# State-space tiles in a frame centred on the 128 double steps, scanned once, and modulation sums by TensorE

## The chip, the cores and the metric

The kernel runs on one core of one Trainium2 chip. The metric is the device time of one execution in microseconds (us); the median of the runs shown is compared.

## The reference, cut to what matters

The model has two layers. Layer 0 mixes tokens with a diagonal complex state-space model (S5), layer 1 with a convolution; each is followed by a SwiGLU feed-forward net. Shift, scale and gate of each sub-layer are sums over the 2048 channels of the condition vector times a weight matrix.

```python
mod = c_act @ ada_w[i] + ada_b[i]                  # six rows of 2048: shift, scale, gate, twice
h = x * (1.0 + sc_m) + sh_m
# S5, for each of 128 groups of 16 channels, with 64 complex states:
a_bar = jnp.exp(lam * dt)
b_bar = ((a_bar - 1.0) / lam)[..., None] * b_mat
h_t = a_bar * h_(t-1) + b_bar @ u_t                # over 256 steps
y = real(c_mat @ h) ; y = gelu(y + d_skip * u)
vg = y @ w_glu ; y = vg[..., :d] * sigmoid(vg[..., d:])
```

The time axis has 256 steps; all matrices are float32.

## The kernel before, in words

**The state-space stage** takes the first part of the execution. A tile `ct` holds 128 channels (8 groups); there are 16 tiles. Two time steps are joined to one double step, so a scan runs over 128 double steps with the factor a_bar squared. A complex scan is made real by turning: with a squared factor of modulus rho and angle w, the input of double step c is multiplied by exp(-i w c), a real scan with rho runs over it, and the result is turned back by exp(i w c). The table of cosines and sines (`tab`) holds 64 entries for each pair of states. So the 128 double steps are cut into two halves `s` of 64, each in its own frame; the end of the first half is turned by 64 steps and added to the first input of the second half. That is the carry: `cx`, `cy`, with the factor `rw` (lines 468 to 477), between the scans of the first half (`step(0)`) and of the second (`step(1)`).

For a tile, `weights_in` turns the input matrices (`mb`, `lz`), `inputs` turns the 128 channels of `x` and applies shift and scale (`u` and `uh`), `drive` multiplies into PSUM (`pin`, 1024 numbers a partition, two banks), and `scan` does the work on VectorE: two multiplies by the table into `x1`, two in place into `pin`, an addition and a subtraction, four scans of 256, the carry, two multiplies into `pc` and two into `psn`. `read_out` multiplies `pc` and `psn` by the output matrices (`mc`) into `y`, after a matmul with the direct term (`bd`, `dd`), and `gelu` follows, in three parts put between the parts of the next scan (`between`). `tables` completes `tab` on GpSimd (POOL) and fills the scan's factors `rho` on ScalarE (ACT).

**Order.** PE's order is written out by hand (`manual_schedule`): in the loop over `ct`, weights of tile ct+1, read-out of tile ct-1, inputs and drive of ct+1, output weights of ct+1, and between them units of the modulation sums. The other engines run in the order that a planner chose when the program was built, each in order at run time.

**Modulation sums.** A unit is 1 MB of `ada_w`, loaded on SyncE's queue into one of six buffers, and multiplied on PE by the condition vector (L632). `plan` gives how many units go into each tile: 4, 4, 2, 2, then 3 for eight tiles, then 4 for four. After four units (two for the first four, narrower blocks) a block of 512 columns is done. Its four partial rows lie on partitions 0, 32, 64 and 96; ACT copies them (`adas`), PE turns each 128 columns by a transpose (`adat`, L640), VectorE sums the four (L643) and adds the bias (L644) into `mod`. Sixteen such blocks fall into this stage. From tile 15 on, the GLU projection's matmuls (L891) follow, with the last scan and the last read-outs between its units.

Of the kernel before, what the change touches and what calls it, by code (L numbers as in the profile page):

```python
# [155 lines left out]
class S5:  # L156
# [8 lines left out]
    def __init__(self, tc, const, ident, psum, psum_tag, psum2):  # L165
        self.psum2 = psum2
        self.tc, self.nc, self.ident = tc, tc.nc, ident
        self.psum, self.ptag = psum, psum_tag
        self.keep_ctx, self.work_ctx, self.mats_ctx = ExitStack(), ExitStack(), ExitStack()
        self.keep = self.keep_ctx.enter_context(tc.tile_pool(name="s5keep", bufs=1))  # L170

        self.cm = self.keep.tile([P, 4, NPAIR, GI], F32, name="cm")

        self.sel = self.keep.tile([P, 4, 2, 32], F32, name="sel")
        for q in range(4):
            self.nc.vector.tensor_copy(out=self.sel[:, q], in_=bc(ident[:, 32 * q:32 * q + 32], 1, 2))
# [5 lines left out]
        self.rw = const.tile([P, 2, NPAIR], F32, name="rw")  # L182
# [5 lines left out]
        self.bd = [w.tile([P, P], F32, name=f"bd{i}") for i in range(3)]  # L188
        self.dd = [w.tile([P, P], F32, name=f"dd{i}") for i in range(3)]
        self.rh = [w.tile([P, 2, 2, 2, 64], F32, name=f"rho{i}") for i in range(2)]  # L190
        for i in range(3):
            for m in (self.mb, self.mc, self.bd, self.rh):
                if i < len(m):
                    self.nc.gpsimd.memset(m[i], 0.0)
# [33 lines left out]
    def turn_mats(self):  # L228

        nc, cm = self.nc, self.cm  # L230
        for q in range(2):
            src = [n.rearrange("p (n i) -> p i n", i=GI) if q == 0 else n.rearrange("p (i n) -> p i n", i=GI)
                   for n in self.nat[2 * q:2 * q + 2]]
            for h in range(4):
                b = self.bank("turn")
                for i in range(4):
                    for r in range(2):
                        k = slice((2 * i + r) * 64, (2 * i + r) * 64 + 64)
                        for a in range(2):
                            nc.tensor.matmul(b[64 * a:64 * a + 64, k], src[r][:, 4 * h + i], self.ident[:, a::2], start=True, stop=True)  # L240
                bv = b.rearrange("p (i r j) -> p r i j", i=4, r=2)
                for r in range(2):
                    nc.scalar.activation(
                        out=cm[:, 2 * q + r, :, 4 * h:4 * h + 4].rearrange("p j i -> p i j"), in_=bv[:, r],
                        func=AF.Copy, scale=-1.0 if q == 1 and r == 1 else 1.0)
                yield

    def prep(self, pp):
# [20 lines left out]
        self.wt = wt[:, 1:]  # L269
# [10 lines left out]
        v.tt(rho, e, e, MUL)  # L280

        for i, l in enumerate((lr, li)):
            g.tt(wt[:, 0, i], l, rec, MUL)
        self.lam = [wt[:, 0, i] for i in range(2)]

    def factors(self):
# [7 lines left out]
        for out, x, y in zip(t, (am1, ai, ai, am1), (lr, li, lr, li)):  # L294
            v.tt(out, x, y, MUL)
        for r in range(2):
            last = v.tt(self.rw[:, r], self.wt[:, 6, r], rho, MUL)
# [4 lines left out]
    def matrices(self, q, engines):  # L302
# [3 lines left out]
        _, cfr, cfi, ar, ai = (bc(self.par[:, i, sl], 2, GI) for i in range(5))  # L306
        u = [keep.tile([P, 16, GI], F32, tag=f"mu{i}", name=f"mu{i}") for i in range(4)]
# [13 lines left out]
        steps = ((c[0:2], (ar, ai), 0, (SUB, ADD)), (c[2:4], (cfr, cfi), 2, (ADD, SUB)), (m[2:4], (ar, ai), 4, (ADD, SUB)))  # L321
# [9 lines left out]
    def quarter(self, q, eng):  # L331
# [3 lines left out]
        for r in range(2):  # L335
            eng.memset(t[:, r, :, 0:1], 1.0 - r)
# [21 lines left out]
    def tables(self, ct, behind=()):  # L358
# [42 lines left out]
    def weights_out(self, ct, skip, behind):  # L401

        nc, k = self.nc, ct % 4
        qc, mb, mc = self.qm[ct // 4][1], self.mb[ct % 2], self.mc[ct % 3]
        dd = self.dd[ct % 3]
# [8 lines left out]
        for r_, end in ((0, False), (1, True)):  # L414
            for p in range(4):
                r = slice(32 * p, 32 * p + 32)
                nc.tensor.matmul(
                    bk[r, 0:32], mb[:, r_, p, 1].rearrange("p a b -> p (a b)"), self.cols(ct, r_, p), start=False, stop=end)
        for p in range(4):
            r = slice(32 * p, 32 * p + 32)  # L420
            nc.scalar.copy(out=self.bd[ct % 3][r, r], in_=bk[r, 0:32])

    def drive(self, ct, u):
# [6 lines left out]
        pin = self.psum2.tile([P, 2, 2, 2, 2, 64], F32, tag="pin", name="pin")  # L430
        for h in range(2):
            for r in range(2):
                for a in range(2):
                    k = slice(64 * a, 64 * a + 64)
                    nc.tensor.matmul(pin[:, a, :, r, h], lz[k, h, r, :], u[k, h], start=h + r == 0, stop=h + r == 2)
        return pin

    def scan(self, ct, pin, tab, between):
# [18 lines left out]
        xf, pf = (z.rearrange("p a s r h c -> p (a s) r (h c)") for z in (x1, pin))
        v.tensor_tensor(out=pf[:, :, 1], in0=xf[:, :, 0], in1=pf[:, :, 1], op=ADD)
        v.tensor_tensor(out=pf[:, :, 0], in0=xf[:, :, 1], in1=pf[:, :, 0], op=SUB)

        def step(s):
            for a in range(2):
                z = pin[:, a, s].rearrange("p r h c -> p (r h c)")
                v.tensor_tensor_scan(out=z, data0=rh[:, a].rearrange("p r h c -> p (r h c)"), data1=z, initial=0.0, op0=MUL, op1=ADD)  # L464

        step(0)
        between()
        cx, cy = (w.tile([P, 2, 2, 2], F32, tag=n, name=n) for n in ("cx", "cy"))
        end = pin[:, :, 0, :, :, 63]
        rw = self.rw[:, :, 4 * ct:4 * ct + 4].rearrange("p k (h a) -> p k a h", a=2)  # L470
        v.tensor_tensor(out=cx, in0=end, in1=bc(rw[:, 0], 2, 2), op=MUL)
        v.tensor_tensor(out=cy, in0=end, in1=bc(rw[:, 1], 2, 2), op=MUL)
        between()
        v.tensor_tensor(out=cx[:, :, 0], in0=cx[:, :, 0], in1=cy[:, :, 1], op=ADD)
        v.tensor_tensor(out=cx[:, :, 1], in0=cx[:, :, 1], in1=cy[:, :, 0], op=SUB)
        first = pin[:, :, 1, :, :, 0]
        v.tensor_tensor(out=first, in0=first, in1=cx, op=ADD)
        between()
        step(1)
        pc, psn = (w.tile([P, 2, 2, 2, 2, 64], F32, tag=n, name=n) for n in ("pc", "psn"))  # L480
        turn(pc, 0)
        between()
        turn(psn, 1)
        return pc, psn

    def read_out(self, ct, u, pc, psn):
# [3 lines left out]
        nc.tensor.matmul(y[:, 0:HALF + 1], self.bd[ct % 3], u[:, 0:HALF + 1], start=True, stop=False)  # L490
        nc.tensor.matmul(y[:, SEQ:SEQ + HALF], self.dd[ct % 3], u[:, HALF:], start=False, stop=False)

        terms = ((0, pc, 1), (1, pc, 0), (2, psn, 0), (1, psn, 1))
        for k, (mi, src, r) in enumerate(terms):
            for tau in range(2):
                ids = {0: (2, 3, 5), 1: (0, 1, 4)}[tau]
                for p in range(4):
# [4 lines left out]
                        y[rr, o:o + HALF].rearrange("p (s c) -> p s c", s=2), self.cols(ct, ids[mi], p), src[:, p % 2, :, r, p // 2],  # L502
                        start=False, stop=tau == 1 and k == 3)
# [4 lines left out]
def kernel(  # L508
# [49 lines left out]
    s5 = S5(tc, const, ident, auxp, "aux", pin_ctx.enter_context(tc.tile_pool(name="pin", bufs=2, space=PSUM)))  # L558
    s5_prep = ExitStack()
# [64 lines left out]
    def ada_block(layer, j, c0, n):  # L624
# [13 lines left out]
        tr = aux("adat")[:, :n]  # L638
# [696 lines left out]
    def inputs(ct):  # L1335
# [445 lines left out]
```

## Time and profile before

| | |
|---|---|
| median of 3 runs | 2293.14 us (2290.69 to 2295.21) |
| the profiled execution | 2298.0 us, its span 2295.8 us |
| granted TensorE clock, mean | 0.992 |
| PE, DVE, ACT, POOL busy | 97%, 74%, 44%, 7% of the span |
| data moved | 579.48 MB, 252 GB/s over the span |

The profile is of one execution. PE is TensorE, DVE VectorE, ACT ScalarE, POOL GpSimd, SP SyncE; L452 is line 452 of the kernel. A tile's name stands for any of its buffers.

### The profile page before, as it was taken

What the parts mean: (1) busy time and instruction counts of PE and PEld (TensorE: products, weight loads), DVE (VectorE), ACT (ScalarE), POOL (GpSimd) and SP (SyncE); (2) the same over time, 40 slices, a digit from 0 to 9 for tenths busy, and PEclk for the clock granted to TensorE, in tenths of its full rate; (3) what the DMA queues carried; (4) which work ended last, traced back from release to release, by engine and by line L of the source; (5) the groups of instructions that cost most, each with busy time, mean ns of one, the idle gap of its engine ahead of it and who ended that gap; (6) DMA issues with size and microseconds to landing.
All of it is one profiled execution on the core that took longest, in us unless ns stands there. A gap on an engine that the chain in (4) does not pass through costs nothing.

```text
span 2295.8 us, 33563 instructions
## 1 busy us (share of the span) xinstructions
PE 2223.8 (97%) x13619; PEld 1799.3 (78%) x13619; DVE 1691.1 (74%) x1941; ACT 1015.6 (44%) x1253; POOL 156.0 (7%) x268
## 2 busy tenths in 40 slices
PE   6888999999999999999999998999999999999999
PEld 4555777987777887787898776898888888888888
DVE  8899888887787777787989788878755444545474
ACT  4665334644334333434446333556443333343343
POOL 5662000000000000000010110000000000000000
PEclk9999999999999999999999999999999999999999
DMA  9889799488998998999866774766875555565542
GB/s 333 288 298 301 270 329 347 161 300 310 321 320 323 325 323 308 324 323 322 307 203 195 213 214 163 276 206 203 291 234 190 188 191 189 184 193 191 185 166 92
DMA packets 380608, 579.48 MB, mean 252 GB/s; under 512 B 13875, under 2 KB 277939, under 8 KB 365987
## 3 DMA queue, kind: packets, MB, share of 16 engines
q1 hardware_dynamic: 379862, 576.82, 74.3%
q8 instruction: 107, 1.75, 0.3%
q0 software_dynamic: 352, 0.45, 0.1%
q14 instruction: 47, 0.39, 0.0%
q10 hardware_dynamic: 240, 0.08, 0.0%
HBM read 573.72 MB, written 3.57 MB: 251 GB/s over the span
## 4 chain that ended last, share of the span: by engine, by line
PE 69%; DVE 13%; DMA 9%; ACT 5%; issue 3%; SPq 0%; POOL 0%; DVEq 0%; ACTq 0%
PE acc L891 55%; PE acc L895 6%; DMA raw<-in_ffn_w_gu_dram 5%; DVE wlo L836 4%; ACT whi L835 3%; DVE adaacc L703 2%; DMA raw<-in_ffn_w_down_dram 2%; PE acc L1007 2%; PE turned L907 1%; PE conv L1672 1%; DMA raw<-in_s_w_glu_dram 1%; DVE pin L464 1%; PE y L501 1%; PE ada L632 1%; DMA raw<-in_ada_w_dram 1%
## 5 line engine op out<-in xcount | busy, mean ns | idle before, releaser
L836 DVE TENSOR_TENSOR wlo<-raw,whi 128x2048 fp32r<-128x2048 f32 x344 | 788.9, 2294 | 462.5 <-ACT whi L835 460.8
L835 ACT CAST whi<-raw 128x2048 fp32r<-128x2048 f32 x344 | 655.6, 1906 | 826.3 <-PE acc L891 407.1
L891 PE MATMUL acc<-whi,h 128*128 128x512 f32 x3648 | 889.2, 393 | 11.3 <-ACT whi L835 11.0
L891 PEld LDWEIGHTS acc<-whi,h 128*128 128x128 f32 x3648 | 677.3, 188 | 166.0 <-ACT whi L835 18.8
L891 PE MATMUL acc<-wlo,h 128*128 128x512 f32 x1824 | 461.7, 390 | 1.0 <-DVE wlo L836 0.9
L891 PEld LDWEIGHTS acc<-wlo,h 128*128 128x128 f32 x1824 | 341.6, 188 | 74.3 <-DVE wlo L836 3.7
L891 PE MATMUL acc<-whi,f 128*128 128x512 f32 x1248 | 300.9, 391 | 0.0
L703 DVE SCALAR_TENSOR_TENSOR adaacc<-rawa,c_act,adaacc 128x2048 f32<-128x2048 f32 (+1 forms) x135 | 284.5, 2107 | 0.4
L891 PEld LDWEIGHTS acc<-whi,f 128*128 128x128 f32 x1248 | 232.8, 188 | 49.5 <-ACT whi L835 1.7
L891 PE MATMUL acc<-wlo,f 128*128 128x512 f32 x624 | 156.4, 389 | 0.0
L891 PEld LDWEIGHTS acc<-wlo,f 128*128 128x128 f32 x624 | 117.1, 188 | 24.3
L1602 POOL TENSOR_TENSOR lw<-fold,wtap 128x1024 f32<-128x1024 f32 x12 | 26.3, 2195 | 1064.1 <-PE acc L895 874.8
L632 PE MATMUL ada<-raw,c_rep 128*32 128x512 f32 (+1 forms) x576 | 71.3, 591 | 5.7 <-DMA raw<-in_ada_w_dram 3.7
L1240 ACT ACTIVATE fsg<-acc 128x256 f32<-128x256 f32 x84 | 31.6, 379 | 96.2 <-PE acc L891 96.2
L895 PE MATMUL acc<-h,whi 128*128 128x256 f32 x512 | 67.3, 286 | 4.2 <-DVE h L1705 2.2
L895 PEld LDWEIGHTS acc<-h,whi 128*128 128x128 f32 x512 | 63.6, 192 | 9.9 <-ACT h L911 4.3
L1184 POOL CAST lnmh<-lno 128x2 fp32r<-128x2 f32 x1 | 0.2, 181 | 885.3 <-DVE lno L68 885.3
L1241 DVE TENSOR_TENSOR fsg<-acc,fsg 128x256 f32<-128x256 f32 x84 | 35.0, 418 | 16.0 <-ACT fsg L1240 16.0
L464 DVE TENSOR_TENSOR_SCAN pin<-rho,pin 128x256 f32<-128x256 f32 x64 | 44.2, 691 | 1.5
L1672 PE MATMUL conv<-vs,lw 128*32 128x256 f32 x720 | 42.2, 380 | 0.1
L895 PE MATMUL acc<-f,whi 128*128 128x256 f32 x320 | 40.7, 284 | 0.0
L895 PEld LDWEIGHTS acc<-f,whi 128*128 128x128 f32 x320 | 39.3, 192 | 0.2
(349 smaller groups left out, 1852.8 us busy)
## 6 DMA issues: line engine op xcount, KB each, us to landing
raw<-in_ffn_w_gu_dram SPq DMA_DIRECT2D x352, 512.0 KB, 4.7
rawa<-in_ada_w_dram SPq DMA_DIRECT2D x128, 1024.0 KB, 5.6
raw<-in_ffn_w_down_dram SPq DMA_DIRECT2D x88, 1024.0 KB, 5.1
raw<-in_ada_w_dram SPq DMA_DIRECT2D x64, 1024.0 KB, 7.6
raw<-in_s_w_glu_dram SPq DMA_DIRECT2D x64, 512.0 KB, 6.1
raw<-in_cv_w_pw_dram SPq DMA_DIRECT2D x64, 512.0 KB, 5.9
raw<-in_cv_w_pw_dram SPq DMA_DIRECT2D x16, 1024.0 KB, 5.9
vs<-scr SPq DMA_DIRECT2D x40, 142.0 KB, 5.5
```

The source lines that it names most:

```text
L464: v.tensor_tensor_scan(out=z, data0=rh[:, a].rearrange("p r h c -> p (r h c)"), data1=z, initial=0.0, op0=MUL, op1=ADD)
L632: nc.tensor.matmul(acc[32 * (k % 4):32 * (k % 4) + 32, :], c_rep[:, kk, :], r[:, k, :], start=kk < 4, stop=kk >= NCH - 4)
L703: nc.vector.scalar_tensor_tensor(out=acc, in0=r[:, i], scalar=c_act[:, kk:kk + 1], in1=acc, op0=MUL, op1=ADD)
L835: m1 = nc.scalar.copy(out=self.hi[:, :kn], in_=r[:, :kn])
L836: m2 = nc.vector.tensor_tensor(out=self.lo[:, :kn], in0=r[:, :kn], in1=self.hi[:, :kn].bitcast(F32), op=SUB)
L891: nc.tensor.matmul(acc[bank].rearrange("p a b -> p (a b)"), x[:, bank * HALF:(bank + 1) * HALF], wt[:, k], start=first, stop=end)
L895: nc.tensor.matmul(acc[bank][:, i], wt[:, k, m * P:(m + 1) * P], x, start=first and i == 0, stop=end and i == 1)
L1007: nc.tensor.matmul(acc[m][:, 0:EW], wt[:, k, m * P:(m + 1) * P], xx[:, 4 * u + k], start=u == 0 and n == 0, stop=u == 3 and n == len(order ...
L1240: nc.scalar.activation(out=t[:, i], in_=gv[:, 0], func=AF.Sigmoid)
L1241: nc.vector.tensor_tensor(out=t[:, i], in0=gv[:, 0], in1=t[:, i], op=MUL)
L1602: nc.gpsimd.tensor_tensor(out=lw, in0=fold32.unsqueeze(1).unsqueeze(1).broadcast_to([P, 4, CONV_G, 32]), in1=bc(wtap[:, :, 4 * (ch + k):4 ...
L1672: nc.tensor.matmul(acc[32 * q:32 * q + 32, :], lw[:, q, g, :], vs[:, q, 4 * g:4 * g + SEQ], start=g == 0, stop=g == n - 1)
```

## The change

One frame serves all 128 double steps. It is centred: double step 64+j has the angle w(j + 1/2), double step 63-j its negative. So the table starts at half a double step (`half`), and the first half of the steps reads the same 64 entries backwards, with the sign of the sine turned. The halves now lie one behind the other (`pin` as [a, h, r, 128]), one scan over 1024 numbers does all, with a zero in the factor row at each start, and the carry and `rw` go. The half-step shift is taken into the input matrices (`ap` in place of `ar`, `ai` in `matrices`) and their channel order (`turn_mats`, `inputs`, `sel`). `mc`, `bd`, `dd` have two buffers instead of three. A modulation block is turned and summed by four matmuls with one moving column (`ada_sel`, ones on partitions 0, 32, 64 and 96), and VectorE's addition reads PSUM. The core of the diff:

```diff
-        self.mc = [w.tile([P, 6, 4, 2, GI], F32, name=f"mc{i}") for i in range(3)]
+        self.mc = [w.tile([P, 6, 4, 2, GI], F32, name=f"mc{i}") for i in range(2)]
...
-        self.rh = [w.tile([P, 2, 2, 2, 64], F32, name=f"rho{i}") for i in range(2)]
+        self.rh = [w.tile([P, 4, 2, HALF], F32, name=f"rho{i}") for i in range(2)]
...
-        v.tt(ar, e, wt[:, 0, 0], MUL)
-        self.ready = v.tt(ai, e, wt[:, 0, 1], MUL)
+        for i in range(2):
+            p, x, y = (z.rearrange(o, a=2, h=2) for z, o in (
+                (self.ap[:, i], "p (t h a) -> p t a h"), (e, "p (t a h) -> p t a h"), (wt[:, 0, i], "p (t a h) -> p t a h")))
+            self.ready = v.tt(p, x, y, MUL)
+        g.tt(ar, e, wt[:, 0, 0], MUL)
+        g.tt(ai, e, wt[:, 0, 1], MUL)
...
-        for r in range(2):
-            last = v.tt(self.rw[:, r], self.wt[:, 6, r], rho, MUL)
...
-        for r in range(2):
-            eng.memset(t[:, r, :, 0:1], 1.0 - r)
+        eng.tensor_copy(out=t[:, :, :, 0], in_=self.half[:, :, sl])
...
-            for r in range(2):
-                nc.scalar.copy(out=rh[:, :, r, :, 1:], in_=bc(self.rho[:, sl].rearrange("p (h a) -> p a h", a=2), 3, 63))
+            nc.scalar.copy(out=rh[:, :, :, 1:], in_=bc(bc(self.rho[:, sl], 2, 2), 3, HALF - 1))
...
         def turn(out, k):
-            for a in range(2):
-                o, i = (z[:, a].rearrange("p s r h c -> p (s r) h c") for z in (out, pin))
-                self.end = v.tensor_tensor(out=o, in0=i, in1=bc(t[:, k, a::2], 1, 4), op=MUL)
...
+            o, i = (z.rearrange("p a h r (s c) -> p (a h) r s c", s=2) for z in (out, pin))
+            if k == 2:
+                for r in range(2):
+                    v.scalar_tensor_tensor(out=o[:, :, r, 0], in0=i[:, :, r, 0], scalar=-1.0, in1=t[:, 1, :, ::-1], op0=MUL, op1=MUL)
+            else:
+                v.tensor_tensor(out=o[:, :, :, 0], in0=i[:, :, :, 0], in1=bc(t[:, k, :, ::-1], 2, 2), op=MUL)
+            self.end = v.tensor_tensor(out=o[:, :, :, 1], in0=i[:, :, :, 1], in1=bc(t[:, min(k, 1)], 2, 2), op=MUL)
...
-        step(0)
         between()
-        cx, cy = (w.tile([P, 2, 2, 2], F32, tag=n, name=n) for n in ("cx", "cy"))
...
-        v.tensor_tensor(out=first, in0=first, in1=cx, op=ADD)
+        z = pin.rearrange("p a h r c -> p (a h r c)")
+        v.tensor_tensor_scan(out=z, data0=rh.rearrange("p q r c -> p (q r c)"), data1=z, initial=0.0, op0=MUL, op1=ADD)
         between()
-        step(1)
...
-        turn(psn, 1)
+        turn(psn, 2)
...
         for b in range(nb):
-            nc.tensor.transpose(tr[:, b * P:(b + 1) * P], part[:, b * P:(b + 1) * P], ident)
-        s = tp.tile([P, 4], F32, tag="adasum", name="adasum")[:, :nb]
+            nc.tensor.matmul(tr[:, b:b + 1], part[:, b * P:(b + 1) * P], ada_sel[:, 0:1], start=b == 0, stop=b == nb - 1)
         with queue_behind([s5.ready]):
-            nc.vector.tensor_reduce(out=s, in_=tr.rearrange("p (b q r) -> p b q r", q=4, r=32)[:, :, :, 0], axis=mybir.AxisListType.X, op=ADD)
-        nc.vector.scalar_tensor_tensor(
-            out=mod[layer][:, j, ch:ch + nb], in0=s, scalar=plus_one(j), in1=ab_col[layer][:, 16 * j + ch:16 * j + ch + nb], op0=ADD, op1=ADD)
+            nc.vector.scalar_tensor_tensor(
+                out=mod[layer][:, j, ch:ch + nb], in0=tr, scalar=plus_one(j), in1=ab_col[layer][:, 16 * j + ch:16 * j + ch + nb], op0=ADD, op1=ADD)
```

## Rows read from the trace of the kernel before

**Rows 1.** the page, part 1: busy time of each engine, share of the span, instructions.

```profile
PE 2223.8 (97%) x13619; PEld 1799.3 (78%) x13619; DVE 1691.1 (74%) x1941; ACT 1015.6 (44%) x1253; POOL 156.0 (7%) x268
```

**Rows 2.** windows; us, PE, PEld, DVE, ACT, POOL busy, clock, DMA share, GB/s.

```profile
44.40:55.20 10.80, 8.37 (x106) 3.96 (x98) 10.02 (x20) 7.71 (x28) 10.64 (x19) 0.88 1.05 386
90.00:120.00 30.00, 26.43 (x421) 16.25 (x414) 28.28 (x58) 19.57 (x59) 19.80 (x43) 0.94 0.81 270
150.00:180.00 30.00, 26.67 (x444) 16.35 (x444) 28.37 (x60) 20.64 (x63) 20.65 (x43) 1.00 0.89 298
230.00:250.00 20.00, 20.00 (x145) 16.36 (x144) 14.76 (x20) 7.89 (x9) 3.02 (x2) 1.00 0.50 167
```

**Rows 3.** timeline of DVE, first carry instruction of tiles 3 and 14: start, us.

```profile
88.39 0.15 DVE L471 TENSOR_TENSOR cx<-pin,rw 128x8 f32<-128x8 f32 x1
...
212.96 0.17 DVE L471 TENSOR_TENSOR cx<-pin,rw 128x8 f32<-128x8 f32 x1
```

**Rows 4.** timeline of DVE, carry to second scan, in two tiles.

```profile
121.70 0.17 DVE L471 TENSOR_TENSOR cx<-pin,rw 128x8 f32<-128x8 f32 x1
...
123.14 0.69 DVE L464 TENSOR_TENSOR_SCAN pin<-rho,pin 128x256 f32<-128x256 f32 x1
...
190.07 0.17 DVE L471 TENSOR_TENSOR cx<-pin,rw 128x8 f32<-128x8 f32 x1
...
190.82 0.69 DVE L464 TENSOR_TENSOR_SCAN pin<-rho,pin 128x256 f32<-128x256 f32 x1
```

**Rows 5.** groups of DVE by line and shape, whole span: busy us, mean ns | idle.

```profile
L464 DVE TENSOR_TENSOR_SCAN pin<-rho,pin 128x256 f32<-128x256 f32 x64 | 44.2, 691 | 1.5
...
L452 DVE TENSOR_TENSOR pin<-pin,tab 128x512 f32<-128x512 f32 x32 | 22.3, 696 | 1.2
...
L1362 DVE SCALAR_TENSOR_TENSOR u<-u,y 128x256 f32<-128x256 f32 x16 | 6.6, 415 | 8.2 <-ACT u L1359 8.1
...
L644 DVE SCALAR_TENSOR_TENSOR mod<-adasum,adab 128x4 f32<-128x4 f32 x14 | 3.9, 281 | 0.0
...
L643 DVE TENSOR_REDUCE adasum<-adat 128x4 f32<-128x16 f32 x14 | 2.3, 164 | 4.3 <-PE adat L640 4.1
```

**Rows 6.** line 1638 of DVE: duration in ns, least, median, most.

```profile
L1638 DVE TENSOR_TENSOR V<-vacc,shift x4: 629/632/641, 1275.5 to 1402.3; 128x256 f32<-128x256 f32 x4
L1638 DVE TENSOR_TENSOR vacc<-vacc,shift x1: 430/430/430, 1416.5 to 1416.5; 128x256 f32<-128x256 f32 x1
```

**Rows 7.** waits in 90 to 210 us: us in total, times, longest.

```profile
PE y L501 <- DVE pc L452: 6.2, 7, 2.4
...
PE bdp L417 <- ACT mc L410: 4.0, 8, 0.5
...
PE adat L640 <- ACT adas L635: 3.5, 4, 1.2
```

**Rows 8.** timeline of PE, read-out to read-out, and a turned block.

```profile
150.01 0.38 PE L490 MATMUL y<-u,bd 128*128 128x129 f32 x1
...
157.15 0.66 PE L640 MATMUL adat<-ident,adas 128*128 128x128 f32 x4
157.73 0.64 PE L632 MATMUL ada<-raw,c_rep 128*32 128x512 f32 x4
...
160.31 0.38 PE L490 MATMUL y<-u,bd 128*128 128x129 f32 x1
...
197.01 0.49 PE L490 MATMUL y<-u,bd 128*128 128x129 f32 x2
...
208.09 0.38 PE L490 MATMUL y<-u,bd 128*128 128x129 f32 x1
```

**Rows 9.** timeline of PE, the two matmuls of hmod.

```profile
130.31 0.61 PE L1332 MATMUL hmod<-mod,sel 128*128 128x8 f32 x4
130.86 0.64 PE L632 MATMUL ada<-raw,c_rep 128*32 128x512 f32 x4
```

**Rows 10.** groups of ACT by line and shape: busy us, mean ns | idle.

```profile
L378 ACT COPY rho<-par 128x252 f32<-128x252 f32 x32 | 11.7, 399 | 5.5 <-DVE pin L464 5.2
```

More of the change, by code (lines that the diff above doesn't have):

```diff
@@ L175, in __init__ @@
         for q in range(4):
-            self.nc.vector.tensor_copy(out=self.sel[:, q], in_=bc(ident[:, 32 * q:32 * q + 32], 1, 2))
+            p = 2 * (q % 2) + q // 2
+            self.nc.vector.tensor_copy(out=self.sel[:, q], in_=bc(ident[:, 32 * p:32 * p + 32], 1, 2))
         self.fold = self.keep.tile([P, 32], F32, name="fold")
@@ L181, in __init__ @@
                 out=self.fold, in0=ident[:, 0:32] if q == 1 else self.fold, in1=ident[:, 32 * q:32 * q + 32], op=ADD)
-        self.rw = const.tile([P, 2, NPAIR], F32, name="rw")
+        self.ap = const.tile([P, 2, NPAIR], F32, name="ap")
         self.qm, self.tq = {}, {}
@@ L239, in turn_mats @@
                         for a in range(2):
-                            nc.tensor.matmul(b[64 * a:64 * a + 64, k], src[r][:, 4 * h + i], self.ident[:, a::2], start=True, stop=True)
+                            o, m = b[64 * a:64 * a + 64, k], self.ident[:, a::2]
+                            if q == 0:
+                                o = o.rearrange("p (t h a) -> p t h a", h=2, a=2)
+                                m = m.rearrange("p (t a h) -> p t h a", h=2, a=2)
+                            nc.tensor.matmul(o, src[r][:, 4 * h + i], m, start=True, stop=True)
                 bv = b.rearrange("p (i r j) -> p r i j", i=4, r=2)
@@ L268, in prep @@
         wt = keep.tile([P, 8, 2, NPAIR], F32, name="wt")
-        self.wt = wt[:, 1:]
+        self.wt, self.half = wt[:, 1:], wt[:, 0]
         re, im = wt[:, 0::2, 0], wt[:, 0::2, 1]
@@ L276, in prep @@
         rho, cfr, cfi, ar, ai = (par[:, i, :] for i in range(5))
-        v.tt(ar, e, wt[:, 0, 0], MUL)
-        self.ready = v.tt(ai, e, wt[:, 0, 1], MUL)
+        for i in range(2):
+            p, x, y = (z.rearrange(o, a=2, h=2) for z, o in (
[3 more added lines that the diff above has]
+        g.tt(ai, e, wt[:, 0, 1], MUL)
         self.rho = rho
         v.tt(rho, e, e, MUL)
+        over = keep.tile([P, 2, 16, 32], F32, tag="tq", name="lq", bufs=2).rearrange("p a b c -> p (a b c)").rearrange("p (a j) -> p a j", j=NPAIR)
         for i, l in enumerate((lr, li)):
-            g.tt(wt[:, 0, i], l, rec, MUL)
-        self.lam = [wt[:, 0, i] for i in range(2)]
+            g.tt(over[:, i], l, rec, MUL)
+        self.lam = [over[:, i] for i in range(2)]
     def factors(self):
@@ L306, in matrices @@
         _, cfr, cfi, ar, ai = (bc(self.par[:, i, sl], 2, GI) for i in range(5))
+        ap = [bc(self.ap[:, i, sl], 2, GI) for i in range(2)]
         u = [keep.tile([P, 16, GI], F32, tag=f"mu{i}", name=f"mu{i}") for i in range(4)]
@@ L417, in weights_out @@
                 nc.tensor.matmul(
-                    bk[r, 0:32], mb[:, r_, p, 1].rearrange("p a b -> p (a b)"), self.cols(ct, r_, p), start=False, stop=end)
+                    bk[r, 0:32], mb[:, r_, 2 * (p % 2) + p // 2, 1].rearrange("p a b -> p (a b)"), self.cols(ct, r_, p), start=False, stop=end)
         for p in range(4):
             r = slice(32 * p, 32 * p + 32)
-            nc.scalar.copy(out=self.bd[ct % 3][r, r], in_=bk[r, 0:32])
+            nc.scalar.copy(out=self.bd[ct % 2][r, r], in_=bk[r, 0:32])
     def drive(self, ct, u):
         nc, lz = self.nc, self.lz[ct % 2]
-        pin = self.psum2.tile([P, 2, 2, 2, 2, 64], F32, tag="pin", name="pin")
+        pin = self.psum2.tile([P, 2, 2, 2, HALF], F32, tag="pin", name="pin")
         for h in range(2):
@@ L434, in drive @@
                     k = slice(64 * a, 64 * a + 64)
-                    nc.tensor.matmul(pin[:, a, :, r, h], lz[k, h, r, :], u[k, h], start=h + r == 0, stop=h + r == 2)
+                    nc.tensor.matmul(pin[:, a, h, r], lz[k, h, r, :], u[k, h], start=h + r == 0, stop=h + r == 2)
         return pin
@@ L455, in scan @@
+            self.end = v.tensor_tensor(out=o[:, :, :, 1], in0=i[:, :, :, 1], in1=bc(t[:, min(k, 1)], 2, 2), op=MUL)
+        x1 = w.tile([P, 2, 2, 2, HALF], F32, tag="x1", name="x1")
         turn(x1, 0)
         turn(pin, 1)
[L457 to L464, printed above, removed]
@@ L476, in scan @@
-        first = pin[:, :, 1, :, :, 0]
-        v.tensor_tensor(out=first, in0=first, in1=cx, op=ADD)
-        between()
-        step(1)
-        pc, psn = (w.tile([P, 2, 2, 2, 2, 64], F32, tag=n, name=n) for n in ("pc", "psn"))
+        xf, pf = (z.rearrange("p a h r (s c) -> p (a h) (r s) c", s=2) for z in (x1, pin))
+        v.tensor_tensor(out=pf[:, :, 0::3], in0=xf[:, :, 2:0:-1], in1=pf[:, :, 0::3], op=ADD)
+        v.tensor_tensor(out=pf[:, :, 1:3], in0=xf[:, :, 3::-3], in1=pf[:, :, 1:3], op=SUB)
@@ L481, in scan @@
+        between()
+        z = pin.rearrange("p a h r c -> p (a h r c)")
+        v.tensor_tensor_scan(out=z, data0=rh.rearrange("p q r c -> p (q r c)"), data1=z, initial=0.0, op0=MUL, op1=ADD)
+        between()
+        pc, psn = (w.tile([P, 2, 2, 2, HALF], F32, tag=n, name=n) for n in ("pc", "psn"))
         turn(pc, 0)
         between()
-        turn(psn, 1)
+        turn(psn, 2)
         return pc, psn
@@ L489, in read_out @@
         y = self.bank("y")
-        nc.tensor.matmul(y[:, 0:HALF + 1], self.bd[ct % 3], u[:, 0:HALF + 1], start=True, stop=False)
-        nc.tensor.matmul(y[:, SEQ:SEQ + HALF], self.dd[ct % 3], u[:, HALF:], start=False, stop=False)
+        nc.tensor.matmul(y[:, 0:HALF + 1], self.bd[ct % 2], u[:, 0:HALF + 1], start=True, stop=False)
+        nc.tensor.matmul(y[:, SEQ:SEQ + HALF], self.dd[ct % 2], u[:, HALF:], start=False, stop=False)
         terms = ((0, pc, 1), (1, pc, 0), (2, psn, 0), (1, psn, 1))
@@ L501, in read_out @@
                     nc.tensor.matmul(
-                        y[rr, o:o + HALF].rearrange("p (s c) -> p s c", s=2), self.cols(ct, ids[mi], p), src[:, p % 2, :, r, p // 2],
-                        start=False, stop=tau == 1 and k == 3)
+                        y[rr, o:o + HALF], self.cols(ct, ids[mi], p), src[:, p // 2, p % 2, r], start=False, stop=tau == 1 and k == 3)
         return y.rearrange("p (t c) -> p t c", t=2)[:, :, :HALF]
@@ L558 @@
     s5 = S5(tc, const, ident, auxp, "aux", pin_ctx.enter_context(tc.tile_pool(name="pin", bufs=2, space=PSUM)))
+    ada_sel = tp.tile([P, 16], F32, name="ada_sel", bufs=1)
+    nc.gpsimd.tensor_copy(out=ada_sel, in_=s5.fold[:, 0:16])
     s5_prep = ExitStack()
```

29 lines of the change are left out of this document (10 added, 19 removed).

## The prediction

> **What bounds the kernel now.** I read the page first: TensorE (PE) is busy 97% of the span, VectorE (DVE) 74% [rows 1], an average over stages. So I asked for windows of the first 230 us, the state-space stage that the change touches. There DVE is busy 28.3 us of 30 and PE 26.5 [rows 2]: two engines nearly full, and the question is which one ends a tile.
>
> The distance between tiles comes from the timeline: the first carry instruction (L471) of tile 3 starts at 88.39 and of tile 14 at 212.96 [rows 3], so eleven tiles take 124.57 us, 11.32 each. Seven of them carry three modulation units of 1 MB on PE, four carry four (the list `plan`).
>
> The chain of waits runs through DVE for much of this stretch, but a chain shows one path, not how near the next one is. So I took PE alone. From one read-out (L490) to the next, PE needs 10.30 us in a three-unit tile and 11.08 in a four-unit tile, both times without a wait for DVE [rows 8]. PE's own pace for the eleven tiles is then 7 x 10.30 + 4 x 11.08 = 116.4; less 1.0, because the three-unit sample holds a turned block (0.58, rows 8) that only three tiles in four have: 115.4 us. A DVE of no cost would gain 124.6 - 115.4 = 9.2 us there, not more. The waits agree: in 90 to 210 us PE waits for DVE's `pc` only 6.2 us in all, and for ACT 3.5 and 4.0 us [rows 7].
>
> **DVE, part by part (per tile).** The carry goes: five instructions, from L471 to the second half's scan 1.44 us where something delays them and 0.75 where nothing does [rows 4]. I take 1.1, the middle.
>
> Four scans of 256 elements (691 ns each, 2.76 in all) become one of 1024. A 256-element scan takes what a 512-element multiply takes (696), so an element of it costs two of the multiply's: (696 - 415)/256 = 1.1 ns doubled [rows 5]. Then 0.691 + 768 x 2.2 ns = 2.38 us, 0.4 less. If the scan had no start cost at all the saving would be nil; I take 0.4.
>
> The two multiplies into `psn` become three instructions, because the minus sign of the first half needs a scalar: 2 x 415 for 256 elements instead of one of 696: +0.13 [rows 5].
>
> The reduce of a modulation block (164 ns) goes and the addition behind it reads PSUM [rows 5]; its mean of 281 lies above the reduce's though it handles as few numbers, so it has been held up, which may end: -0.16 to -0.3 per block.
>
> Sum: -1.1 - 0.4 + 0.13 - 0.2 = -1.6 us, so DVE's tile falls from at most 11.3 to about 9.7. That is below PE's 10.3 and 11.08, so DVE stops ending tiles.
>
> Now half of each table multiply reads the table backwards: 512 elements in four groups, 2048 per tile. No row here reads backwards. The nearest rows are the shift in the convolution: 430 ns where only the read jumps at every element, 632 where the write jumps as well [rows 6], against 415 for a plain form of the size. Bounds: nothing, or (632 - 415)/256 = 0.85 ns each, 1.7 us per tile. A backward read is a read without jumps, nearest to 430, so I take nothing and keep 1.7. [...]
>
> **PE.** Transposes of a modulation block become matmuls with one moving column. In the records a transpose is one entry (four for a block of four [rows 8]), an ordinary matmul two (four for two [rows 9]). Four transposes take 0.58 from start to the next instruction [rows 8]; the `hmod` pair, two matmuls with 128x128 weights and few columns, takes 0.55 [rows 9]. So four matmuls take 1.1: +0.5 us per block of four, about +0.2 for the four blocks of two. The change that is to spare work puts it on the engine that comes next. The eleven tiles hold 37 units, 9.25 blocks: +4.6 us. Were a matmul of one column as short as a transpose it would be nothing. Drive, read-out and input matmuls keep their number and columns; only their order of channels changes.
>
> **ACT, POOL and the rest.** The factor rows become one copy of 1016 elements instead of two of 252 at 399 ns [rows 10]: between 0.8 and 1.6 us, so up to +0.8. ACT is busy 19.6 of 30 us [rows 2], so it fits; but it runs in order, and behind such a copy stand the copies that PE waits for [rows 7]. I charge nothing, for the unit of modulation that PE has between the inputs and the drive covers it; without that cover it is up to 0.8 x 11 = 9 us. Two buffers instead of three for `mc`, `bd` and `dd`: the one rewritten for tile ct+1 was read by read-out ct-1, which PE issues ahead of the inputs on which those ACT copies wait, so no wait is added. Start: two small products move to POOL, the first column of a table is a copy instead of two memsets, two products for `rw` go, the memsets change size; each is some tenths of a us beside DMA-bound work (DMA share 1.05, rows 2), counted as nothing. SP's issues and their order stay; the weight loads wait for PE to free buffers and come as much sooner as PE does.
>
> **Sum.** Steady tiles: -9.2 + 4.6 = -4.6 us. First four tiles and their seven blocks: DVE saves about 1.6 on each, but DMA and PE hold part of that stretch and the blocks cost PE 4 x 0.2 + 2.75 x 0.5 = 2.2; I take -1.4. Last tile: PE is busy 20.00 of 20 us at 230 to 250 [rows 2], so nothing. Total -6.0. The profiled execution took 2298.0 us for a span of 2295.8, the median of the runs is 2293.14; taken off the first, 2292.0, and off the median, which is what is forecast, 2287.1, say **2287**. Less than 0.2% (4.6 us) is about what a measurement here can't tell from no change, so this stands close to it.
>
> **Rivals.**
> 1. *PE gains on all counts* (17%): a one-column matmul costs no more than a transpose, and the waits for ACT shrink with DVE's, since ACT's in-order copies stand behind DVE. For it: 7.5 us of ACT waits. Against: `hmod`. Gain 9.2 + 1.4 + 2.2 to 16: 2277 to 2281.
> 2. *No gain to be seen* (18%): ACT's longer copy or the DMA stream takes the place of DVE. DMA is 0.81 and 0.89 busy [rows 2], which leaves 11% or more, against a wish of 4% (4.6 us of 124.6). Half the gain gone: 2289 to 2293.
> 3. *Backward reads are slow* (9%): 1.7 us per tile put DVE back at 11.4, above PE and level with before: 11 x 0.1 = +1; 2292 to 2296. [...]
> 4. *Slower through the modulation sums* (6%): PE's order is fixed, so if DVE's time isn't what ends tiles, twelve blocks at 0.5 and four at 0.2 lengthen the stage by 6.8 us: 2299.9. It decides once less than 6.8 of the 9.2 + 1.4 us comes back. The 6.2 us of waits for `pc` is just under that point; the waits behind ACT and the low clock at idle (0.94 at 90 to 120 us, rows 2) should carry it over.
>
> **How the numbers follow.** My forecast, PE takes over, has 50%: 2283 to 2290. The range from 2277 to 2295 leaves out most of 4, the worst of 3 and a DVE that would set the end alone (16 x 1.6 = 26 us, which PE's pace excludes). Faster by over 0.2% (below 2288.5): rival 1 and two thirds of the forecast, with a little of 2: 52%. Slower (above 2297.7): 4 and some of 2 and 3: 10%. Within: 38%.
>
> **What would show it.** One scan of about 2.35 us per tile; table multiplies still near 0.69; eight entries for four modulation matmuls, 1.1 us in all; PE waiting for `pc` near zero while its busy share in 90 to 190 us rises; DVE idle over 1 us per tile; tiles some 10.9 us apart; ACT's factor copy near 1.0. Wrong if the multiplies stretch beyond 0.8, if PE still waits for `pc`, or if later stages change their own length.

## The result, and the profile after

The changed kernel took 2299.72 us (median of 11 runs, 2295.47 to 2306.83) beside 2293.14 of the kernel before (11 runs, 2290.11 to 2299.39): a ratio of 1.0032 with a 95% interval of 1.0018 to 1.0045. The forecast was 2287 with a range up to 2295. So it is slower by 0.3%, and the number lies where rival 4 put it. The profiled execution is one of its quicker ones (2298.96 us for a span of 2296.8, only 1.0 above the profiled execution of before), so what follows is read from the state-space stage, where the two traces differ in place, and not from the spans.

The page, part 1 of the changed kernel, answers to [rows 1]: PE has 13.8 us more, DVE 19.5 less.

```profile
PE 2237.6 (97%) x13683; PEld 1814.5 (79%) x13683; DVE 1671.6 (73%) x1808; ACT 1019.6 (44%) x1237; POOL 157.2 (7%) x266
```

DVE did what the diff says. The groups of DVE and ACT by line and shape in the changed kernel (busy us, mean ns | idle), which answer to [rows 5, 10]:

```profile
L472 DVE TENSOR_TENSOR_SCAN pin<-rho,pin 128x1024 f32<-128x1024 f32 x16 | 36.7, 2292 | 0.4
L459 DVE SCALAR_TENSOR_TENSOR psn<-pin,tab 128x256 f32<-128x256 f32 x32 | 12.4, 414 | 0.0
L461 DVE TENSOR_TENSOR x<-pin,tab 128x512 f32<-128x512 f32 x16 | 10.9, 683 | 4.4 <-PE pin L441 3.5 <-POOL qb L324 0.9
L462 DVE TENSOR_TENSOR x<-pin,tab 128x512 f32<-128x512 f32 x16 | 10.9, 680 | 0.0
L637 DVE SCALAR_TENSOR_TENSOR mod<-adat,adab 128x4 f32<-128x4 f32 x14 | 2.2, 160 | 11.9 <-PE adat L635 11.8
L384 ACT COPY rho<-par 128x1016 f32<-128x1016 f32 x16 | 16.6, 1038 | 0.2
```

L461 reads the table backwards and L462 forwards: 683 and 680 ns. The idle time at L637 grew: DVE now stands idle 11.8 us for PE's modulation sums, where the reduce stood idle 4.1 us for PE's transposes before [rows 5].

Windows of the changed kernel answer to [rows 2]; the columns are the same, and the one to look at is the third from the right, the granted clock.

```profile
90.00:120.00 30.00, 28.53 (x457) 17.51 (x450) 26.68 (x40) 22.69 (x64) 24.78 (x48) 0.94 0.95 318
150.00:180.00 30.00, 26.51 (x360) 15.07 (x356) 25.72 (x40) 19.85 (x59) 16.51 (x35) 0.89 0.80 263
180.00:210.00 30.00, 25.27 (x344) 14.48 (x344) 22.44 (x36) 16.38 (x46) 8.57 (x16) 0.91 0.81 283
```

The last of these windows in the kernel before:

```profile
180.00:210.00 30.00, 26.54 (x404) 14.73 (x400) 28.36 (x62) 18.31 (x56) 8.23 (x15) 1.00 0.89 309
```

DVE is down from 28.4 to 25.7 and 22.4 us of 30, as meant. But from 150 to 210 us TensorE's clock, which was 1.00 before, is 0.89 and 0.91. In slices of 1 us of this stretch of the trace it reads 1.00 or 0.50, and something between (0.63 to 0.99) only in a slice in which it changes, so a mean of 0.90 says that some 12 of these 60 us (twice 0.10 of 60) ran at 0.50.

The waits in 90 to 210 us (engine, line, waited for: us in total, times, longest), which answer to [rows 7]:

```profile
PE adat L635 <- ACT adas L630: 6.3, 5, 1.6
DVE mod L637 <- PE adat L635: 6.2, 6, 1.6
...
PE bdp L423 <- ACT mc L416: 4.0, 8, 0.5
```

PE's wait for `pc`, 6.2 us before, is gone, and its wait for ACT's copy of a finished modulation block (`adas`) rose from 3.5 to 6.3. What stands behind that wait is seen in PE's timeline of the changed kernel (start, us, instruction, entries, which are the records of it in the trace, and in brackets the idle time before it and its releaser), which answers to [rows 8]:

```profile
191.53 0.66 PE L404 MATMUL btr<-ident,mb 128*128 128x128 f32 x4
193.82 1.17 PE L635 MATMUL adat<-ada_sel,adas 128*128 128x1 f32 x8 [1.64 <-ACT adas L630]
194.93 1.93 PE L627 MATMUL ada<-raw,c_rep 128*32 128x512 f32 x8
196.79 0.80 PE L484 MATMUL y<-u,bd 128*128 128x129 f32 x2
197.38 0.64 PE L485 MATMUL y<-u,dd 128*128 128x128 f32 x2
```

PE idles 1.64 us, spends 1.1 us on four matmuls of one column, and then eight entries of a modulation unit take 1.93 us, at a clock of 0.50 (194.93 to 196.79). Where the clock is not lowered (1.00 in 182.16 to 183.16) the same eight entries take 1.07:

```profile
181.18 1.05 PE L635 MATMUL adat<-ada_sel,adas 128*128 128x1 f32 x8 [1.63 <-ACT adas L630]
182.16 1.07 PE L627 MATMUL ada<-raw,c_rep 128*32 128x512 f32 x8
183.16 0.49 PE L484 MATMUL y<-u,bd 128*128 128x129 f32 x2
```

That block too stood behind a wait of 1.63 us, so the fall does not come every time. Of the nine blocks from 90 to 210 us five stood behind a wait for `adas`; the unit behind them took 1.93 us or more three times, 1.62 once, and 1.07 once. And behind one of the four blocks without a wait the unit took 1.27 us:

```profile
151.94 1.05 PE L635 MATMUL adat<-ada_sel,adas 128*128 128x1 f32 x8
152.92 1.27 PE L627 MATMUL ada<-raw,c_rep 128*32 128x512 f32 x8
```

Where the time went is read from the starts of the read-outs (L484; L490 before) in the same timelines, read-outs 8 and 15 of the changed kernel and read-out 15 of the kernel before (its read-out 8 is in [rows 8]):

```profile
144.81 0.49 PE L484 MATMUL y<-u,bd 128*128 128x129 f32 x2
243.28 0.39 PE L484 MATMUL y<-u,bd 128*128 128x129 f32 x2
...
238.58 0.39 PE L490 MATMUL y<-u,bd 128*128 128x129 f32 x2
```

Read-out 8 starts at 144.81 us against 150.01 before: 5.2 ahead. Read-out 15, the last, starts at 243.28 against 238.58: 4.7 behind. So 9.9 us were lost between them, in the stretch of the lowered clock. It also holds six blocks that each take 0.40 us more (0.98 from start to the next instruction, where the transposes took 0.58), 2.4 in all. The stages after it, whose code is the same, took 2053.5 us from there to the end of the span in this profile and 2057.2 before: the profiled execution hides part of what the medians show. In the ten kernels of this document that rest took between 2046.0 and 2058.4 us, one profile each, with the same code. So a single profile settles what happened in the stage, and not the total.

### The profile page after: what moved, and what is told of

It is laid out like the page before. It is cut to its first block, busy times and chain, and to the rows that moved or that the text cites. A ratio compares the mean times of both kernels' runs of the same rounds, so it can differ in the third digit from the quotient of the medians.

```text
span 2296.8 us, 33538 instructions
## 1 busy us (share of the span) xinstructions
PE 2237.6 (97%) x13683; PEld 1814.5 (79%) x13683; DVE 1671.6 (73%) x1808; ACT 1019.6 (44%) x1237; POOL 157.2 (7%) x266
## 4 chain that ended last, share of the span: by engine, by line
PE 80%; DVE 8%; ACT 5%; DMA 5%; issue 2%; POOL 0%; SPq 0%; DVEq 0%; ACTq 0%
PE acc L884 63%; PE acc L888 5%; DMA raw<-in_ffn_w_gu_dram 3%; DVE wlo L829 2%; PE acc L1000 2%; PE turned L900 2%; ACT whi L828 2%; PE ada L627 1%; PE y L495 1%; DMA raw<-in_s_w_glu_dram 1%; PE conv L1665 1%; DVE adaacc L696 1%; PE adat L635 1%; PE xt L1337 0%; ACT uh L940 0%
## 5 line engine op out<-in xcount | busy, mean ns | idle before, releaser
L627 PE MATMUL ada<-raw,c_rep 128*32 128x512 f32 (+1 forms) x576 | 76.8, 634 | 2.3 <-POOL qc L324 1.6
L472 DVE TENSOR_TENSOR_SCAN pin<-rho,pin 128x1024 f32<-128x1024 f32 x16 | 36.7, 2292 | 0.4
```

What stands on the lines that cost most here:

```text
L472: v.tensor_tensor_scan(out=z, data0=rh.rearrange("p q r c -> p (q r c)"), data1=z, initial=0.0, op0=MUL, op1=ADD)
L627: nc.tensor.matmul(acc[32 * (k % 4):32 * (k % 4) + 32, :], c_rep[:, kk, :], r[:, k, :], start=kk < 4, stop=kk >= NCH - 4)
```

## The experiments

The theory: the frame and the single scan gain about what the prediction gave DVE; the modulation sums by one-column matmuls lose more than that, and the larger part of their loss is TensorE's clock, because PE now does next to nothing while it waits for `adas` and right behind it. Two rivals: the frame is what costs (backward reads, ACT's longer copy); or it is the sums, but by their length on PE alone. Each expectation, quoted as it stood ahead of its run, names its own theories by letters. Each ratio below is to the kernel before on the same chip, whose median was 2291.05 us beside both kernels of experiment 1, the first of experiment 2 and that of experiment 3, and 2289.98 beside the other four.

**1. The two halves of the change, each alone.** The first kernel is the changed one with the sums as before:

```diff
-            nc.tensor.matmul(tr[:, b:b + 1], part[:, b * P:(b + 1) * P], ada_sel[:, 0:1], start=b == 0, stop=b == nb - 1)
+            nc.tensor.transpose(tr[:, b * P:(b + 1) * P], part[:, b * P:(b + 1) * P], ident)
...
+            nc.vector.tensor_reduce(out=s, in_=tr.rearrange("p (b q r) -> p b q r", q=4, r=32)[:, :, :, 0], axis=mybir.AxisListType.X, op=ADD)
...
```

> The centred frame and the single scan alone: the modulation blocks are turned by transposes and summed by VectorE again, as before. Theory A (the sums on TensorE cost the time: 0.47 us more per block, and TensorE's clock falls behind them): this gains what DVE's waits cost TensorE before, 3 to 8 us, so 2285 to 2290 us, with the granted clock at 150 to 210 us back near 1.00 from 0.89 to 0.91. Theory B (the frame's own side effects cost it: the factor copy of 1.04 us and the new order on ACT hold back the copy that TensorE waits for): it stays at 2297 to 2302 us, TensorE waits some 1.6 us for that copy in the last tiles and the clock stays low.

Measured: 2281.35 us, ratio 0.9961 [0.9946, 0.9976], 3.6 us below the range of theory A. The second is the kernel before with only the sums changed (the same lines, the other way round).

> The modulation sums on TensorE alone, everything else as before. Theory A: slower than before by 4 to 9 us, 2297 to 2302 us, with a lower granted clock in 150 to 210 us. Theory B: within 2 us of before, 2291 to 2295 us, since DVE still sets the pace of the tiles and hides 0.47 us per block.

Measured: 2298.58 us, ratio 1.0027 [1.0017, 1.0038], in the range of theory A. So it is not the frame that costs: it gains 0.39%, and the sums alone lose about as much as the whole change. Windows of the kernel with the frame alone:

```profile
90.00:150.00 60.00, 55.98 (x924) 33.66 (x926) 58.74 (x96) 46.72 (x134) 48.04 (x96) 1.00 0.95 328
150.00:210.00 60.00, 50.40 (x726) 29.83 (x717) 52.98 (x82) 38.98 (x105) 20.63 (x40) 0.97 0.89 293
```

and of the one with the sums alone:

```profile
90.00:150.00 60.00, 53.93 (x792) 32.43 (x788) 54.40 (x115) 40.46 (x124) 37.66 (x71) 0.94 0.83 279
150.00:210.00 60.00, 52.85 (x792) 31.43 (x788) 52.21 (x111) 37.06 (x114) 26.56 (x53) 0.94 0.86 297
```

The frame alone has nearly the same wait for `adas` (5.6 us in 90 to 210), and from 90 us on its clock stays up behind the blocks; the 0.97 comes from its second half (1.00 in 150 to 180 us, 0.94 in 180 to 210), where the GLU projection starts at 204.67 us behind a wait of 2.56 us for ACT, and its first 16 entries take 5.53 us, where 16 at 214.73 us take 3.94. PE's timeline, with the transposes:

```profile
180.57 0.66 PE L633 MATMUL adat<-ident,adas 128*128 128x128 f32 x4 [1.64 <-ACT adas L628]
181.15 1.06 PE L625 MATMUL ada<-raw,c_rep 128*32 128x512 f32 x8
```

**2. Length or clock.** The changed kernel, with 128 equal moving columns in place of one: more columns for PE, the same sums.

```diff
-            nc.tensor.matmul(tr[:, b:b + 1], part[:, b * P:(b + 1) * P], ada_sel[:, 0:1], start=b == 0, stop=b == nb - 1)
+            nc.tensor.matmul(tr[:, b * P:(b + 1) * P], part[:, b * P:(b + 1) * P], ada_sel[:, 0:1].broadcast_to([P, P]), start=b == 0, stop=b == nb - 1)
...
```

> The changed kernel, but each modulation matmul has 128 moving columns (the same column 128 times) instead of one. Theory A1 (the clock falls because TensorE does next to nothing during these matmuls): the clock at 150 to 210 us comes back to 0.97 or more and the time falls to 2290 to 2297 us, although each block takes some 0.25 us longer. Theory A2 (only the length of the matmuls counts) or B (ACT's order): the clock stays at 0.9 and the time is 2300 to 2305 us.

Measured: 2287.08 us, ratio 0.9987 [0.9977, 0.9996], with the clock of theory A1 and 2.9 us below its range. A block became no shorter (1.16 us against 1.05), PE waits as long for `adas` (6.7 us in 90 to 210), and yet the kernel is 12.6 us quicker than the changed one by the two medians, 10.3 by the two ratios (0.45% of 2291). The window and a block of it:

```profile
150.00:210.00 60.00, 52.43 (x810) 32.08 (x810) 49.93 (x80) 38.30 (x111) 22.41 (x42) 1.00 0.84 287
```

```profile
190.16 1.16 PE L635 MATMUL adat<-ada_sel,adas 128*128 128x128 f32 x8 [1.22 <-ACT adas L630]
191.24 1.07 PE L627 MATMUL ada<-raw,c_rep 128*32 128x512 f32 x8
```

The same edit in the old frame, on the kernel with the sums alone:

> The modulation sums by TensorE alone, in the old frame, each matmul with 128 equal moving columns instead of one. One column gave 2298.6 against 2291.1 before, at a granted clock of 0.87 in 0 to 90 us and 0.94 in 150 to 210. Theory A (the loss is mainly the clock): 2289 to 2294, windows of the clock no lower than before's. Rival B (the loss is the longer PE time of a block, 16 blocks x 0.5): 2297 to 2301, as with one column.

Measured: 2288.71 us, ratio 0.9994 [0.9983, 1.0004], level with before and 0.3 us below the range of theory A. The mean clock of the stage is back (0.97; 0.96 before), though not in every window: from 150 to 210 us it is 0.98, where it was 1.00 before.

```profile
90.00:150.00 60.00, 51.84 (x794) 31.08 (x790) 56.73 (x116) 40.10 (x121) 38.39 (x72) 1.00 0.86 290
150.00:210.00 60.00, 53.38 (x806) 32.87 (x798) 54.26 (x112) 37.72 (x115) 28.41 (x57) 0.98 0.82 283
```

So length alone is not the cause. In the old frame, where DVE is the fuller engine, the longer block costs nothing that can be measured, and the loss of the sums goes with the clock.

**3. Wait and short matmuls apart.** The changed kernel, with a finished block's sum taken behind the next read-out instead of at the next unit, which was meant to give ACT's copy time to end:

```diff
         if block and not block[1]:
-            next(block[0], None)
+            summed.append(block[0])
             block = None
...
+        if not wait:
+            while summed:
+                next(summed.pop(0), None)
...
-            ada_units(n > 0)
+            ada_units(n > 0, True)
...
                 y = s5.read_out(*held)
+            ada_turn()
```

> The changed kernel, but a block that is complete at the end of a tile is turned behind the next read-out instead of ahead of the next unit, so that ACT's copy has some 4 us more. Theory B: TensorE's waits for that copy (6.3 us in 90 to 210 us) go, the gaps close, the clock recovers, 2285 to 2292 us. Theory A: the matmuls keep their 1.05 us per block and the clock falls with them, 2296 to 2302 us.

Measured: 2287.13 us, ratio 0.9986 [0.9974, 0.9998], with a clock of 1.00 in 150 to 210 us. Two of its waits in 90 to 210 us:

```profile
PE ada L627 <- ACT adas L630: 5.9, 5, 1.6
...
DVE mod L637 <- PE adat L635: 2.7, 4, 1.0
```

The time and the clock are those of theory B, but its reason did not hold, so neither theory holds as it was written. The wait did not go: `ada`, in which a block is summed up, has one bank, so the next unit waits for the same copy. The one-column matmuls are unchanged too (250 ns the median record in both kernels). What changed is that they no longer stand behind each other, and the time came back. Other matmuls stand around both now as well, so this run does not show which part of the new order did it.

**4. More work ahead of the short matmuls.** The changed kernel with four transposes of the identity, whose results nothing uses, issued before the sums:

```diff
-        tr = aux("adat")[:, :nb]
+        bank = aux("adat")
+        for b in range(4):
+            nc.tensor.transpose(bank[:, b * P:(b + 1) * P], ident, ident)
+        tr = bank[:, :nb]
```

> The whole change, with four transposes of the identity (128 columns each, some 0.6 us, results not used) put on PE ahead of the one-column matmuls of every block, so that PE does more work, partly in the time in which it would wait for ACT's copy. Theory A (the clock falls because PE does next to nothing in the wait and in the one-column matmuls behind it): faster than the whole change in spite of the added work, 2286 to 2294, granted clock 0.97 or more in 150 to 210 us. Rival B (it is the time of the block on PE that counts): 16 blocks x up to 0.58 more than the whole change's 2299.7, 2300 to 2309.

Measured: 2293.38 us, ratio 1.0005 [0.999, 1.0019]: 0.27% below the changed kernel's ratio, with more work on PE. Its window, and a block of it:

```profile
150.00:210.00 60.00, 53.77 (x790) 33.86 (x782) 48.98 (x76) 37.98 (x108) 25.85 (x51) 0.97 0.81 283
```

```profile
191.05 0.60 PE L635 MATMUL adat<-ident 128*128 128x128 f32 x4
192.86 1.05 PE L638 MATMUL adat<-ada_sel,adas 128*128 128x1 f32 x8 [1.22 <-ACT adas L630]
193.85 1.06 PE L627 MATMUL ada<-raw,c_rep 128*32 128x512 f32 x8
```

The theory of the clock held, at the edge of its range; the two intervals touch, and the transposes also fill part of the wait for `adas` (3.8 us of it are left in 90 to 210), so this run alone would not decide.

**5. The later sum on the best kernel, and ACT's copy.** The frame alone with the later sum of experiment 3:

> The frame and the one scan alone, with the modulation sums by transposes and a reduce as before, and with a finished block's sum taken behind the next read-out instead of at the next unit. The frame alone gave 2281.4 us and the whole change with the later sum 2287.1. Theory A (the wait for ACT's copy of a finished block is only moved, because the block's accumulator has one bank; what the later sum gave back in the whole change was the clock, which transposes don't lower): level with the frame alone, 2279 to 2285, PE's clock 0.97 to 1.00 in 90 to 210 us. Rival B (the wait itself was worth the 12.6 us): 2268 to 2275.

Measured: 2285.8 us, ratio 0.9984 [0.9975, 0.9993]. The wait itself was not worth the time that came back in experiment 3. The kernel is even 0.23% above the frame alone, 0.8 us beyond the range of theory A; its clock was 0.86 in the first 90 us (0.91 in the frame alone) and 0.98 and 1.00 behind them. Why the early clock is lower was not followed. The frame alone with ACT's copy of the scan's factors issued twice:

```diff
             nc.scalar.copy(out=rh[:, :, :, 1:], in_=bc(bc(self.rho[:, sl], 2, 2), 3, HALF - 1))
+            nc.scalar.copy(out=rh[:, :, :, 1:], in_=bc(bc(self.rho[:, sl], 2, 2), 3, HALF - 1))
```

> The frame and the one scan alone, with ACT's copy of the scan's factors (1.04 us per tile) issued twice, so that ACT has 1.04 us more per tile. Theory A (the copy is covered by the modulation unit that PE runs meanwhile, as the prediction charged it): 2279 to 2285, level with the frame alone (2281.4). Rival B (ACT's copies are on the path that sets the tiles, so the copy eats what the frame gains): 11 to 16 tiles x 1.04, 2292 to 2298.

Measured: 2283.5 us, ratio 0.9976 [0.9966, 0.9985], in the range of theory A. 16 copies, 16.6 us more on ACT, cost 0.15% (3.4 us) by the two ratios, whose intervals overlap: the copy is hidden for the most part.

The runs together; the clock is the mean granted over the first 240 us of the profile, the last column the start of the last read-out there.

```
kernel                                ratio   95% interval       clock   last read-out
before                                1       -                  0.96    238.58
the whole change                      1.0032  1.0018 to 1.0045   0.91    243.28
frame alone                           0.9961  0.9946 to 0.9976   0.96    225.77
sums alone                            1.0027  1.0017 to 1.0038   0.92    245.30
whole change, 128 columns             0.9987  0.9977 to 0.9996   0.96    236.82
sums alone, 128 columns               0.9994  0.9983 to 1.0004   0.97    239.27
whole change, later sum               0.9986  0.9974 to 0.9998   0.96    232.32
whole change, transposes ahead        1.0005  0.9990 to 1.0019   0.95    240.74
frame alone, later sum                0.9984  0.9975 to 0.9993   0.94    233.16
frame alone, factor copy twice        0.9976  0.9966 to 0.9985   0.96    229.16
```

Every kernel that was measured slower has a clock of 0.91 or 0.92 in this stage, and no other has one. That column is of one execution each, but the record has the mean clock of every execution over its whole length, and these agree: on average it is 0.986 in the changed kernel and 0.990 with the sums alone, 0.992 before, and 0.991 to 0.994 in each of the others (0.994 in both kernels with 128 columns). The version that beats both is the frame with the old sums: 0.9961 of before, 0.7% below the whole change by the two ratios.

## Why the prediction was wrong

**DVE's tile: right.** The scan takes 2.29 us (2.38 forecast), the split `psn` 2 x 414 ns, the addition of a block 160 ns where reduce and addition took 445, within the forecast saving. DVE is busy 100.46 us in 90 to 210, and eleven tiles (scan of tile 3 at 84.12 to scan of tile 14 at 209.15) take 125.03, so 9.5 us of DVE per tile; 9.7 was forecast. But the tiles are 11.37 us apart by these scans, where 10.9 was to be seen and 11.32 was before: DVE no longer ended them, and something else held them as long.

**Backward reads at nothing: right.** 683 against 680 ns, where up to 1.7 us per tile had been kept as a bound. These rows show none of it: read backwards, the table took what it took forwards, and rival 3 is out.

**PE's pace as what would be left: right in the frame alone, from samples that were off both ways.** There the gain can be read without the new sums. Read-outs 3, 10 and 13 of the frame alone, and 3 and 10 of the kernel before (its 13 is in [rows 8]):

```profile
87.26 0.49 PE L484 MATMUL y<-u,bd 128*128 128x129 f32 x2
157.65 0.49 PE L484 MATMUL y<-u,bd 128*128 128x129 f32 x2
193.67 0.49 PE L484 MATMUL y<-u,bd 128*128 128x129 f32 x2
...
90.68 0.49 PE L490 MATMUL y<-u,bd 128*128 128x129 f32 x2
171.58 0.49 PE L490 MATMUL y<-u,bd 128*128 128x129 f32 x2
```

From read-out to read-out, which is how the prediction measured PE, a three-unit tile takes 10.06 us on average (read-outs 3 to 10) and was 11.56 before; a four-unit tile takes 12.01 (read-outs 10 to 13) and was 12.17. The prediction had taken one sample of each, 10.30 and 11.08; the second was the shortest of the three four-unit tiles of before. Over the run the frame gained 0.39%, 8.9 us; 9.2 + 1.4 had been the wish for the two stretches.

**The length of a block on PE: right.** Eight entries, 1.05 us, where 1.1 was forecast, and 0.40 more than the transposes took to the next instruction, where 0.5 was. PE's waits for `pc` went as said.

**The sum: wrong, in the term for the modulation sums.** This is the step that failed: it gave a block +0.5 us of PE and nothing else. In the new frame the longer blocks cost 0.26% with 128 columns (0.9987 against 0.9961, 6.0 us), near the 6.8 that rival 4 had summed up for all of them, so their length was sized about right. What was missing is TensorE's clock, 0.91 in the stage with one column and 0.96 with 128: 0.45% more (10.3 us) with one. So the sum was -8.9 for the frame, +6.0 for the length and +10.3 for the clock, 7.4 us, where -9.2 + 4.6 - 1.4 had been put. The clock's arithmetic can be followed in the second half of the stage. The read-outs 8 and 15 with 128 columns, and the windows behind 210 us of the changed kernel and of this one:

```profile
144.34 0.49 PE L484 MATMUL y<-u,bd 128*128 128x129 f32 x2
236.82 0.39 PE L484 MATMUL y<-u,bd 128*128 128x129 f32 x2
...
210.00:240.00 30.00, 26.94 (x282) 20.53 (x279) 22.84 (x28) 13.93 (x24) 4.28 (x12) 0.92 0.79 250
...
210.00:240.00 30.00, 26.94 (x253) 21.22 (x253) 19.06 (x22) 13.71 (x19) 4.27 (x12) 0.94 0.79 249
```

From read-out 8 to read-out 15 the changed kernel needs 98.47 us (144.81 to 243.28), with 128 columns 92.48 (144.34 to 236.82): 6.0 us. Its clock there was 0.90 for 60 us and 0.92 for 30, against 1.00 and 0.94: twice the differences, 12 and 1.2, makes 13.2 us more at a clock of 0.50, if it has the same two levels in both kernels; at 0.50 a unit takes almost twice as long (1.93 against 1.07 us), so the estimate from these numbers is 6.6 us at most. The two profiles are 6.5 us apart at the last read-out. What the 10.3 us hold beyond that is not seen in the stage; behind it, where the code is the same, the profiles differ by 2053.5 against 2047.9 us, within the scatter named above, and this was not followed. The read-outs agree on the cost (6.0 us of 13.2), and 128 moving columns took the mean from 0.91 to 0.96; how a wait and four one-column matmuls lower the clock, no run shows.

**"The low clock at idle should carry it over": wrong in sign.** The prediction read 0.94 in 90 to 120 us as something that a busier PE would mend, and so set 6% on rival 4. The frame alone does mend it (1.00 in 90 to 150). But the prediction only asked how long the new matmuls are, and not what the clock does with one column (0.91 in the stage, 0.96 with 128), nor that they often stand behind a wait for ACT (four times in 120 us before [rows 7], five after). Rival 4 named the right number, 2299.9, by luck: its sum has lengths alone and a frame that gains nothing, while the frame gains 8.9 us, and of what the sums cost on top of it (0.26 + 0.45%) the larger part by these middle values went with the clock.

**"The waits behind ACT should carry it over": wrong.** PE's wait for `adas` grew from 3.5 to 6.3 us instead. With transposes in the same frame it is 5.6, and with the one-column sums in the old frame 3.1; with 128 columns it is 6.7 in the new frame and 5.0 in the old:

```profile
PE adat L642 <- ACT adas L637: 5.0, 5, 1.5
```

So it is longer in the new frame in each pair, but the frame is not all of it. That part of a tile made shorter for DVE comes back as this wait is likely and was not tested.

**ACT's copy and the two buffers: right.** The copy takes 1.04 us and is hidden but for a small part (experiment 5). PE's wait for `mc` is 4.0 us before and after, so two buffers add none that the trace shows; they were not put back by themselves.

What stays open: why the clock falls behind some blocks and not behind others with the same wait (1.63 us and 1.07 behind it at 181 us, 1.64 and 1.93 at 194 us); why the longer blocks cost 5.7 us by the medians and 11 by the profiles (last read-outs 236.82 and 225.77), of which a fall of the clock near 121 us in the 128-column profile (0.94 in 120 to 150 us, 1.00 in the frame alone), where a block takes 1.92 us instead of 1.16, is one part; and why the early clock is lower with transposes and the later sum (0.86 against 0.91 in the first 90 us).

## What to carry to other kernels

Price an instruction on TensorE by its length and also by the granted clock of the instructions behind it (here a unit took 1.07 us at 1.00 and 1.93 at 0.50): read the clock of the stretch, and ask whether the engine waits there and what it does next. A change that replaces transposes or wide matmuls by one-column ones near a wait is a suspect (here the clock of 150 to 210 us was 0.97 with transposes and 0.90 with one column, in the same frame), and the test is cheap: the same matmuls with more columns, or the same wait with something else behind it. And when a change joins two edits, time each alone: here one was worth -0.39%, and the other took it back and 0.32% more.

## What the runs showed of the hardware

Four matmuls of one moving column took 1.05 us and four of 128 equal columns 1.16, so the narrow ones save 0.11 us, while the mean clock of the stage went from 0.91 to 0.96 with the wide ones. PE's transposes kept the clock up as wide matmuls do (a stage mean of 0.96 in the frame alone, with the same longest wait of 1.6 us). In 150 to 210 us a wait of up to 1.64 us with transposes behind it left the clock at 0.97 (the four units behind transposes took 1.06 us each), and one-column matmuls moved away from the wait left it at 1.00; in the changed kernel, with both together, it was 0.90. That is a mean over the blocks and no rule for one of them: behind one block with a wait of 1.63 us the clock did not fall (the unit took 1.07 us), and behind one without it did (1.27 us, at a clock of 0.79).
